# Summing weighted rows on VectorE ahead of one matmul per 512 columns, in the modulation rows of a two-block kernel

## The chip, the cores and the metric

The kernel runs on one core of one Trainium2 chip. The metric is the device time of one execution in microseconds; "before" is the median of three runs. The profile is one further execution, recorded by the hardware profiler. Engines are named as the profile does: PE (matrix multiply), DVE (VectorE), ACT (ScalarE), POOL (GpSimd), SP (the engine that issues most transfers here).

## The reference

A first block of two hybrid layers is followed by a second block (gated linear attention, a state space mixer, a gated recurrence and a feed-forward net). The change touches only the adaptive layer norm of the first block:

```
mod = jax.nn.silu(c) @ ada_w + ada_b          # c: [1, 1024], ada_w: [1024, 3072] per layer
shift, scale, gate = jnp.split(mod, 3, axis=-1)
h = rms_norm(x, norm_g) * (1.0 + scale[:, None, :]) + shift[:, None, :]
proj = h @ w_in
...
return x + gate[:, None, :] * y
```

So for each layer one vector of 1024 numbers is multiplied with a matrix of 1024 x 3072, in float32, giving one row of 3072. Layer 0's shift and scale are computed at the start of the kernel by other code. What is left for later is the gate of layer 0 (1024 columns) and the whole row of layer 1 (3072 columns): eight pieces of 512 columns.

## The kernel before

`ada_rows` (lines 260 to 297) makes the eight later pieces. It returns a list of small jobs, one for each "round" and each block `k` of 128 rows of the matrix: layer 0's gate is one round of 8 jobs with one load each, layer 1 has a round of 8 jobs with two loads each and one of 8 jobs with one load each, 32 loads of 128x1024 (512 KB) in all. A job loads its block into the tile `adaw` (two buffers, line 283) and multiplies each half of 512 columns with the column `self.sc[:, k:k+1]` (128 entries of silu(c)) as a matmul with one output row (line 285). The eight matmuls of a piece accumulate in a PSUM tile `adr`, on partition 32*g. In the last job of a round the row is read by VectorE, the bias is added (line 292), for layer 1's scale also the gain is applied (line 294), and the row goes to DRAM (line 296). Two later matmul records in the profile stand for each float32 matmul.

`hybrid` (from line 402) hands these jobs to layer 0 only (`prep`). They are put one after each job of the second projection stage: chunk "NV" (8 tiles of 128 tokens), "DV" (8 tiles, 256 columns) and "DQ" (8 tiles, 512 columns). A DQ tile (`job_df`, line 744) is 24 matmuls into `pj`, a copy `dr` by ScalarE (three buffers), squares, a sum (line 758), an inverse square root in three Newton steps on VectorE (lines 117 to 123), a scaling (line 762), a rotation in four operations on VectorE for one half and on POOL for the other (`rope`, lines 340 to 343), four transposes on PE into `dfTp` (line 770), and a split into two parts by ScalarE and VectorE (`sgd`, line 774) that goes to DRAM (`dfT`).

After this come the sixteen gate tiles (`gate_tile`, line 605): 24 matmuls into `pg`, a tanh on ScalarE into `gth` (line 612; three buffers), a multiply on VectorE that reads `pg` again (line 613), and a store to `gTd` by SP. `pj` and `pg` share one PSUM tag of two banks. Then attention loads its operands (`md`, line 920, and `ml`, line 866) and starts.

The program's order on each engine is not the order of the code: a scheduler places instructions by its own estimate of their times, and each engine then runs its queue strictly in that order. A weight block is loaded into `raw`, rounded by ScalarE into `wh`, and the rest `wl` is subtracted by VectorE for even blocks and by POOL for odd ones (`load_wt`, lines 153 to 163).

Of the kernel before, what the change touches and what calls it, by code (L numbers as in the profile page):

```python
# [12 lines left out]
F32 = mybir.dt.float32  # L13
# [3 lines left out]
ALU = mybir.AluOpType  # L17
# [35 lines left out]
class Kern:  # L53
# [206 lines left out]
    def ada_rows(self, li, pool, tag, dst, nbuf, rnds=(0, 1)):  # L260

        nc, a = self.nc, self.a
        X = {}

        def step(rnd, k):
            ng = 4 if rnd == 0 else 2
            if k == 0:
                X["p"] = self.ps(tag, f"adr{rnd}")[:, 0:512]
                X["b"] = pool.tile([128, 512], F32, name="brow", tag="brow", bufs=1)
                X["rows"] = pool.tile([128, 512], F32, name="rows", tag="rows", bufs=1)  # L270
                for g in range(ng):
                    ci = rnd * 4 + g
                    nc.scalar.dma_start(X["b"][32 * g:32 * g + 1, :], a["ada_b"][li:li + 1, ci * 512:ci * 512 + 512])
                if rnd == 0:
                    X["n"] = pool.tile([128, 512], F32, name="ngr", tag="ngr", bufs=1)
                    for g in range(2):
                        nc.scalar.dma_start(X["n"][64 + 32 * g:65 + 32 * g, :],
                                            a["norm_g"][li:li + 1, g * 512:g * 512 + 512])
            pr = X["p"]
            for h in range(0, ng, 2):  # L280
                w = pool.tile([128, 1024], F32, name="adaw", tag="adaw", bufs=nbuf)
                c0 = (rnd * 4 + h) * 512
                nc.sync.dma_start(w, a["ada_w"][li, k * 128:(k + 1) * 128, c0:c0 + 1024])
                for g in (h, h + 1):
                    nc.tensor.matmul(pr[32 * g:32 * g + 1, :], self.sc[:, k:k + 1],
                                     w[:, (g - h) * 512:(g - h + 1) * 512], start=k == 0, stop=k == 7)
            if k < 7:
                return
            rows = X["rows"]
            for g in range(ng):  # L290
                sl = slice(32 * g, 32 * g + 1)
                nc.vector.tensor_tensor(rows[sl, :], pr[sl, :], X["b"][sl, :], ALU.add)
                if rnd == 0 and g >= 2:
                    nc.vector.scalar_tensor_tensor(rows[sl, :], rows[sl, :], 1.0, X["n"][sl, :], ALU.add, ALU.mult)
                ci = rnd * 4 + g
                nc.scalar.dma_start(dst[ci:ci + 1, :], rows[sl, :])
        return [lambda r=r, k=k: step(r, k) for r in rnds for k in range(8)]

    def mod_bc(self, pool, mod, which, name):
# [2118 lines left out]
```

## Time and profile before

| | |
|---|---|
| median of 3 runs | 2950.08 us (2942.32 to 2954.98) |
| profiled execution | 2954.67 us, span 2952.9 us |
| PE busy | 2734.3 us (93%) |
| VectorE busy | 1924.0 us (65%) |
| ScalarE busy | 1299.9 us (44%) |
| POOL busy | 1114.3 us (38%) |
| the jobs' matmuls | 128 records, 251.1 to 386.2 us |
| last gate tile of layer 0 | tanh at 427.19 us |

The page gives shares over the whole span; the change lies in a stretch of some 180 us near its start. For that stretch one asks the trace for busy times by window, for the queue of one engine in order of time, and for what each instruction waited for (the square brackets at the end of a row). A matmul record can be longer than the distance to the next one, since matmuls are pipelined; distances between starts are what a matmul costs.

### The profile page before, as it was taken

Reading aid. Unit: us, or ns where it says so; the run is one execution under the profiler, and the core shown is the slowest. Engines: PE = TensorE matmul, PEld = TensorE weight load, DVE = VectorE, ACT = ScalarE, POOL = GpSimd, SP = SyncE. Lnnn points to the kernel's source line nnn. Section 1 sums busy time; section 2 is a strip of 40 time slices with the busy share of each in tenths; the row PEclk is TensorE's granted clock in tenths of the full one; section 3 lists DMA queues with packets and bytes.
Section 4 is the critical chain, followed back from the end, with each engine's and each line's share of the span. In section 5 each row is a group of like instructions: output and inputs, shape, how many; then the busy total and the mean of one; then the engine's idle time right before and its main releaser. Section 6 shows DMA issues by size and latency. Waiting matters only on the chain. (4 is left out here: it accounts for less than half of the span.)

```text
span 2952.9 us, 42552 instructions
## 1 busy us (share of the span) xinstructions
PE 2734.3 (93%) x14954; PEld 2186.5 (74%) x14954; DVE 1924.0 (65%) x4245; ACT 1299.9 (44%) x2542; POOL 1114.3 (38%) x849
## 2 busy tenths in 40 slices
PE   7999999998998999989999998999995989999899
PEld 6987666666778997766767775798673767787687
DVE  4784628785577677267865568643678888776733
ACT  5552227675623643166766323224233323333544
POOL 2232216662221324145742114342204665333743
PEclk9999999999999999989999998899996999999899
DMA  7456661435573363434056742235521555323963
GB/s 225 113 135 211 206 177 69 107 91 151 181 264 99 89 179 100 140 107 117 27 148 187 247 125 71 85 108 193 174 99 64 185 193 188 107 97 124 318 194 109
DMA packets 316602, 428.66 MB, mean 145 GB/s; under 512 B 36658, under 2 KB 224162, under 8 KB 314980
## 3 DMA queue, kind: packets, MB, share of 16 engines
q1 hardware_dynamic: 294464, 367.96, 41.4%
q10 hardware_dynamic: 21924, 57.98, 5.1%
q8 instruction: 118, 1.93, 0.3%
q14 instruction: 96, 0.79, 0.1%
HBM read 292.60 MB, written 132.64 MB: 144 GB/s over the span
## 5 line engine op out<-in xcount | busy, mean ns | idle before, releaser
L794 ACT ACTIVATE P<-P,nb 128x1024 f32<-128x1024 f32 (+1 forms) x320 | 316.5, 990 | 122.8 <-DVE nb L787 94.1
L127 PE MATMUL pj<-wh,hh 128*128 128x384 f32 (+3 forms) x768 | 265.4, 347 | 1.1 <-ACT cr L624 0.5
L128 PE MATMUL pj<-wl,hh 128*128 128x384 f32 (+3 forms) x768 | 264.2, 345 | 0.0
L129 PE MATMUL pj<-wh,hl 128*128 128x384 f32 (+3 forms) x768 | 261.7, 345 | 0.0
L806 PE MATMUL ptp<-ident,P 128*128 128x128 f32 x1568 | 220.3, 279 | 10.0 <-ACT PT L808 6.3
L806 PEld LDWEIGHTS ptp<-ident,P 128*128 128x128 f32 x1568 | 182.0, 143 | 52.0 <-issue 19.9
L954 POOL TENSOR_TENSOR P<-P,cf 128x1024 f32<-128x1024 f32 x64 | 121.8, 1906 | 211.7 <-DVE cf L952 164.6
L2035 POOL TENSOR_TENSOR fwl<-wraw,fwh 128x1024 fp32r<-128x1024 f32 (+1 forms) x66 | 150.2, 2278 | 134.1 <-ACT fwh L2034 126.9
L162 POOL TENSOR_TENSOR wl<-raw,wh 128x384 fp32r<-128x384 f32 (+3 forms) x64 | 77.3, 1212 | 296.7 <-ACT wh L161 253.7
L808 ACT COPY PT<-ptp 128x512 f32<-128x512 f32 (+1 forms) x255 | 138.1, 554 | 72.8 <-PE ptp L806 55.8
L787 DVE CUSTOM_DVE_ANT_0 P<-sd,zero 128x1024 f32<-128x1024 f32 x128 | 153.8, 1216 | 22.0 <-PE sd L945 21.8
L127 PE MATMUL po<-wh,yh 128*128 128x512 f32 x384 | 153.2, 406 | 8.6 <-ACT yh L1548 4.9
L129 PE MATMUL po<-wh,yl 128*128 128x512 f32 x384 | 151.9, 402 | 3.7 <-DVE yl L1549 3.7
L128 PE MATMUL po<-wl,yh 128*128 128x512 f32 x384 | 154.2, 402 | 0.8 <-DVE wl L140 0.5
L955 POOL TENSOR_TENSOR P<-P 128x1024 f32<-128x1024 f32 x64 | 153.5, 2401 | 3.6
L128 PEld LDWEIGHTS pj<-wl,hh 128*128 128x128 f32 x768 | 146.9, 191 | 10.7 <-issue 6.0
L127 PEld LDWEIGHTS pj<-wh,hh 128*128 128x128 f32 x768 | 146.9, 191 | 8.1 <-issue 0.9
L129 PEld LDWEIGHTS pj<-wh,hl 128*128 128x128 f32 x768 | 145.5, 190 | 8.0 <-issue 3.5
L2034 ACT CAST fwh<-wraw 128x512 fp32r<-128x512 f32 (+1 forms) x110 | 86.7, 791 | 142.1 <-PE fu L128 74.5
L787 DVE CUSTOM_DVE_ANT_0 P<-sm,zero 128x1024 f32<-128x1024 f32 x96 | 116.9, 1218 | 48.0 <-PE sm L129 42.8
L2253 DVE TENSOR_TENSOR dxl<-drx,dxh 128x512 fp32r<-128x512 f32 x75 | 77.3, 1054 | 100.3 <-ACT dxh L2252 94.4
L2253 POOL TENSOR_TENSOR dyl<-dry,dyh 128x512 fp32r<-128x512 f32 x75 | 109.5, 1475 | 87.6 <-ACT dyh L2252 87.5
(698 smaller groups left out, 7750.3 us busy)
## 6 DMA issues: line engine op xcount, KB each, us to landing
adaw<-in_ada_w_dram SPq DMA_DIRECT2D x48, 512.0 KB
wraw<-in_w_up_dram SPq DMA_DIRECT2D x22, 1024.0 KB
raw<-in_w_in_dram SPq DMA_DIRECT2D x76, 256.0 KB
drx<-fx SPq DMA_DIRECT2D x75, 256.0 KB
mn<-naT SPq DMA_DIRECT2D x72, 256.0 KB
nab<-in_na_rpb_dram SPq DMA_DIRECT2D x24, 576.0 KB
naT<-sgn SPq DMA_DIRECT2D x64, 192.0 KB
md<-dfT SPq DMA_DIRECT2D x96, 128.0 KB
```

The source lines that it names most:

```text
L127: mm(o, lh, rh, start=first, stop=False, **kw)
L128: mm(o, lh, rl, start=False, stop=False, **kw)
L129: mm(o, ll, rh, start=False, stop=last, **kw)
L787: nc.vector.tensor_tensor_reduce(out=P[:, :n], in0=src, in1=self.zero.to_broadcast([128, n]), op0=ALU.add, op1=ALU.min, scale=1.0, scalar= ...
L794: nc.scalar.activation(P[:, :n], P[:, :n], AF.Exp, bias=nb, scale=-1.0 if bias is None else 1.0, accum_out=sums)
L806: nc.tensor.transpose(T[:, j * 128:(j + 1) * 128], P[:, (c + j) * 128:(c + j + 1) * 128], self.ident)
L808: e(PT[:, c:c + m, q, :], T[:, 0:m * 128].rearrange("p (k t) -> p k t", k=m))
L954: nc.gpsimd.tensor_tensor(Ps[1], Ps[1], cf[:, 1:2].to_broadcast([128, S]), ALU.mult)
L955: nc.gpsimd.tensor_tensor(Ps[0], Ps[0], Ps[1], ALU.add)
L2034: nc.scalar.copy(wh, raw)
L2035: (eng or nc.gpsimd).tensor_tensor(wl, raw, wh.bitcast(F32), ALU.subtract)
L2253: eng.tensor_tensor(lo, raw, hi.bitcast(F32), ALU.subtract)
```

## The change

Each loaded block is multiplied by its 128 entries of `self.sc` on VectorE, one number for each partition, and summed into a tile `adac` of 128x1024: the first block of a round by a product, the next seven by a multiply-and-add. When a round's eight blocks are summed, one matmul with a column of ones for each 512 columns sums over the 128 partitions. `adac` has two buffers of 4 KB a partition. The loads, their buffers and what follows the row are the same.

```diff
+                X["a"] = [pool.tile([128, 1024], F32, name="adac", tag="adac", bufs=2) for _ in range(0, ng, 2)]
             pr = X["p"]
             for h in range(0, ng, 2):
                 w = pool.tile([128, 1024], F32, name="adaw", tag="adaw", bufs=nbuf)
                 c0 = (rnd * 4 + h) * 512
                 nc.sync.dma_start(w, a["ada_w"][li, k * 128:(k + 1) * 128, c0:c0 + 1024])
-                for g in (h, h + 1):
-                    nc.tensor.matmul(pr[32 * g:32 * g + 1, :], self.sc[:, k:k + 1],
-                                     w[:, (g - h) * 512:(g - h + 1) * 512], start=k == 0, stop=k == 7)
+                z = X["a"][h // 2]
+                if k == 0:
+                    nc.vector.tensor_scalar_mul(z, w, self.sc[:, 0:1])
+                else:
+                    nc.vector.scalar_tensor_tensor(z, w, self.sc[:, k:k + 1], z, ALU.mult, ALU.add)
             if k < 7:
                 return
+            for g in range(ng):
+                nc.tensor.matmul(pr[32 * g:32 * g + 1, :], self.ones, X["a"][g // 2][:, g % 2 * 512:g % 2 * 512 + 512],
+                                 start=True, stop=True)
```

In the changed file the lines behind this place are six higher (the gate multiply, 613 before, is 619). Three places show how the order moved.

VectorE, in the middle of the DQ tiles, before: the end of one tile's Newton steps, its rotation, and the next tile's sum.

```order
L762 TENSOR_TENSOR dr<-dr,rsd 128x512
L340 TENSOR_TENSOR rp_u<-dr,cg_dq 128x256
L341 TENSOR_TENSOR rp_w<-dr,sg_dq 128x8x16
L342 TENSOR_TENSOR rp_w<-dr,sg_dq 128x8x16
L758 TENSOR_REDUCE std<-jkd 128x16
L343 TENSOR_TENSOR dr<-rp_u,rp_w 128x256
L117 TENSOR_SCALAR std<-std 128x16
L118 TENSOR_SCALAR rsd<-std 128x16
```

VectorE, a rotation among the DQ tiles in the changed kernel (`adac` is the sum, `csc` the column of silu(c)).

```order
L289 SCALAR_TENSOR_TENSOR adac<-adaw,csc,adac 128x1024
L346 TENSOR_TENSOR rp_u<-dr,cg_dq 128x256
L347 TENSOR_TENSOR rp_w<-dr,sg_dq 128x8x16
L348 TENSOR_TENSOR rp_w<-dr,sg_dq 128x8x16
L123 SCALAR_TENSOR_TENSOR rsd<-nwt,rsd 128x16
L121 TENSOR_TENSOR nwt<-rsd 128x16
L289 SCALAR_TENSOR_TENSOR adac<-adaw,csc,adac 128x1024
L349 TENSOR_TENSOR dr<-rp_u,rp_w 128x256
```

The accumulations stand between the steps of one tile's rotation. Of the 32, eight stand ahead of the first DQ sum and 24 between it and the last rotation.

PE, where the gate tiles have begun, before: matmuls of the gates with one tile's transposes and two groups of the jobs' matmuls between them.

```order
L285 MATMUL adr_3097<-adaw,csc 1x512 x2
L770 MATMUL dfTp<-ident,dr 128x128 x4
L129 MATMUL pg<-hh,wl 128x512
L127 MATMUL pg<-hh,wh 128x512
L128 MATMUL pg<-hl,wh 128x512
L129 MATMUL pg<-hh,wl 128x512
L285 MATMUL adr_3097<-adaw,csc 1x512 x2
```

PE, the end of the second gate tile and the start of the third in the changed kernel.

```order
L129 MATMUL pg<-hh,wl 128x512
L776 MATMUL dfTp<-ident,dr 128x128 x8
L293 MATMUL adr_3453<-adac,ones 1x512 x2
L776 MATMUL dfTp<-ident,dr 128x128 x4
L127 MATMUL pg<-hh,wh 128x512
```

The last three DQ tiles' transposes now stand together behind two whole gate tiles, and all other gate matmuls behind them.

VectorE at the end of the same stretch, before: the last tile's rotation and split, and the first gate multiplies.

```order
L762 TENSOR_TENSOR dr<-dr,rsd 128x512
L340 TENSOR_TENSOR rp_u<-dr,cg_dq 128x256
L341 TENSOR_TENSOR rp_w<-dr,sg_dq 128x8x16
L342 TENSOR_TENSOR rp_w<-dr,sg_dq 128x8x16
L343 TENSOR_TENSOR dr<-rp_u,rp_w 128x256
L774 TENSOR_TENSOR sgd<-dfTp,sgd 128x512
L613 SCALAR_TENSOR_TENSOR gth<-gth,pg 128x512 x2
L774 TENSOR_TENSOR sgd<-dfTp,sgd 128x512
```

VectorE there in the changed kernel.

```order
L768 TENSOR_TENSOR dr<-dr,rsd 128x512
L298 TENSOR_TENSOR rows<-adr_3453,brow 1x512 x2
L346 TENSOR_TENSOR rp_u<-dr,cg_dq 128x256
L347 TENSOR_TENSOR rp_w<-dr,sg_dq 128x8x16
L348 TENSOR_TENSOR rp_w<-dr,sg_dq 128x8x16
L349 TENSOR_TENSOR dr<-rp_u,rp_w 128x256
L780 TENSOR_TENSOR sgd<-dfTp,sgd 128x512
L619 SCALAR_TENSOR_TENSOR gth<-gth,pg 128x512 x7
```

The last round's bias is now added ahead of the last rotation, and the gate multiplies begin only behind the last tile's split; before, two of them stood ahead of it.

SP, the loads for attention among the stores of the gate tiles, before.

```order
L158 DMA raw<-in_w_in_dram 128x512
L614 DMA gTd_86<-gth 128x512
L920 DMA md<-dfT_88 32x1024 x24
L866 DMA ml<-qTd_84 96x1024 x2
L866 DMA ml<-kTd_85 96x1024 x2
L614 DMA gTd_86<-gth 128x512 x7
```

SP, the same loads in the changed kernel.

```order
L284 DMA adaw<-in_ada_w_dram 128x1024 x4
L782 DMA dfT_88<-sgd 128x4x128 x6
L926 DMA md<-dfT_88 32x1024 x24
L872 DMA ml<-qTd_84 96x1024 x2
L872 DMA ml<-kTd_85 96x1024 x2
L620 DMA gTd_86<-gth 128x512 x7
```

All stores of gate tiles now stand behind the 28 loads; before, eight of the sixteen stood ahead of them.

## Rows read from the trace of the kernel before

**Rows 1.** The page, busy time of the engines, with share and instructions.

```profile
PE 2734.3 (93%) x14954; PEld 2186.5 (74%) x14954; DVE 1924.0 (65%) x4245; ACT 1299.9 (44%) x2542; POOL 1114.3 (38%) x849
```

**Rows 2.** Busy time by window, layer 0; columns as the first row says.

```profile
core 0: us, PE busy (x) PEld busy (x) DVE busy (x) ACT busy (x) POOL busy (x), PEclk, DMA share, GB/s
290.00:330.00 40.00, 40.00 (x177) 24.79 (x175) 36.67 (x104) 12.59 (x22) 18.94 (x24) 1.00 0.76 227
```

**Rows 3.** Instructions on tile adr: count, nanoseconds (least, median, most), first and last start.

```profile
L285 PE MATMUL adr<-adaw,csc x128: 590/591/592, 251.1 to 386.2; 128*1 128x512 f32 x128
```

**Rows 4.** PE in order of time: start, length, engine, line, operation, tiles, count.

```profile
250.77 0.28 PE L128 MATMUL pj<-wl,hh 128*128 128x256 f32 x1
250.89 0.28 PE L129 MATMUL pj<-wh,hl 128*128 128x256 f32 x1
251.10 1.03 PE L285 MATMUL adr<-adaw,csc 128*1 128x512 f32 x4
...
252.28 0.28 PE L128 MATMUL pj<-wl,hh 128*128 128x256 f32 x1
```

**Rows 5.** DVE in order of time, layer 1's DQ tiles; brackets: idle before, releaser.

```profile
1129.76 0.69 DVE L758 TENSOR_REDUCE std<-jkd 128x16 f32<-128x512 f32 x1 [5.42 <-ACT jkd L756]
...
1183.88 0.56 DVE L343 TENSOR_TENSOR dr<-rp_u,rp_w 128x256 f32<-128x256 f32 x1
...
1186.43 0.69 DVE L774 TENSOR_TENSOR sgd<-dfTp,sgd 128x512 fp32r<-128x512 f32 x1 [0.19 <-ACT sgd L773]
```

**Rows 6.** Busy time by window, layer 1's DQ tiles.

```profile
1130.00:1140.00 10.00, 10.00 (x45) 8.26 (x44) 9.80 (x36) 1.85 (x3) 4.27 (x7) 1.00 0.00 1
...
1160.00:1170.00 10.00, 7.04 (x33) 5.19 (x32) 9.62 (x22) 3.06 (x7) 5.99 (x6) 1.00 0.33 89
```

**Rows 7.** DVE groups by form: count, busy us, mean ns, idle before.

```profile
L1615 DVE SCALAR_TENSOR_TENSOR rgm<-rgm,rtr 128x1024 f32<-128x1024 f32 x12 | 14.6, 1220 | 0.2
...
L1597 DVE SCALAR_TENSOR_TENSOR xc<-xr,convw,xc 128x1024 f32<-128x1024 f32 x6 | 10.5, 1754 | 0.1
...
L209 DVE TENSOR_SCALAR xs<-xs,xrs 128x1024 f32<-128x1024 f32 x4 | 2.8, 751 | 0.1
```

**Rows 8.** SP in order of time, the third and fourth load.

```profile
252.16 2.79 SPq L283 DMA_DIRECT2D adaw<-in_ada_w_dram  x2
```

**Rows 9.** Busy time by window beside it; the last number is GB/s, or KB.

```profile
253.00:254.00 1.00, 1.00 (x10) 0.52 (x8) 0.00 (x0) 0.00 (x0) 0.00 (x0) 1.00 0.69 143
254.00:255.00 1.00, 1.00 (x8) 0.49 (x5) 0.07 (x1) 0.00 (x0) 0.00 (x0) 1.00 0.91 356
```

**Rows 10.** DVE in order of time, layer 0's first DQ sum.

```profile
269.16 0.69 DVE L758 TENSOR_REDUCE std<-jkd 128x16 f32<-128x512 f32 x1 [4.41 <-ACT jkd L756]
```

**Rows 11.** Instructions on tile rows, the bias additions.

```profile
L292 DVE TENSOR_TENSOR rows<-adr,brow x8: 672/683/697, 280.5 to 387.6; 1x512 f32<-1x512 f32 x8
```

**Rows 12.** ACT in order of time, tanh of gate tiles, layer 0 and layer 1.

```profile
427.19 0.60 ACT L612 ACTIVATE gth<-pg 128x512 f32<-128x512 f32 x1 [4.84 <-PE pg L129]
...
1193.29 0.60 ACT L612 ACTIVATE gth<-pg 128x512 f32<-128x512 f32 x1 [6.89 <-PE pg L129]
...
1212.29 0.60 ACT L612 ACTIVATE gth<-pg 128x512 f32<-128x512 f32 x1 [7.53 <-DMA gTd<-gth]
...
1264.02 0.60 ACT L612 ACTIVATE gth<-pg 128x512 f32<-128x512 f32 x1 [4.85 <-PE pg L129]
```

**Rows 13.** SP in order of time, layer 1's loads for attention and the stores behind.

```profile
1190.27 11.83 SPq L920 DMA_DIRECT2D md<-dfT  x24
...
1204.46 12.25 SPq L614 DMA_DIRECT2D gTd<-gth  x5
```

**Rows 14.** DVE in order of time, two 16-column operations in layer 0.

```profile
316.41 0.17 DVE L117 TENSOR_SCALAR std<-std 128x16 f32<-128x16 f32 x1
316.62 1.24 DVE L118 TENSOR_SCALAR rsd<-std 128x16 int32<-128x16 int32 x1
```

**Rows 15.** POOL in order of time, beside them.

```profile
316.53 3.07 POOL L162 TENSOR_TENSOR wl<-raw,wh 128x512 fp32r<-128x512 f32 x2 [2.08 <-ACT wh L161]
```

## The prediction

> **What bounds the kernel now.** I read the page first, then stage windows, then single queues. PE is busy for 93% of the span [rows 1], and in the stage of the change it has no gap: from 290 to 330 us it is busy 40.00 of 40 us, but VectorE is busy 36.67 of 40 in the same stretch [rows 2]. The reader should see both numbers, since the work goes from the first engine to the second just there. The stage is layer 0's last projections: eight "DV" tiles, eight "DQ" tiles (24 matmuls each, then a long VectorE chain that scales and rotates the tile) and sixteen gate tiles. The 64 one-column matmuls leave 128 records there [rows 3].
>
> A control stands in the same trace. Layer 1 runs the same tiles with no modulation work beside them. There the first reduction of the DQ chain starts at 1129.76 and the last rotation ends at 1183.88 + 0.56 = 1184.44, which is 54.7 us [rows 5]; VectorE is busy 9.80 and 9.62 of 10 us in two of these slices, and PE only 7.04 of 10 in the second [rows 6]. So with the modulation matmuls gone, this stretch is already VectorE's. In layer 0 those matmuls lie in time that PE would else partly wait. That is the base of the forecast.
>
> **What is removed and added on PE.** Ordinary matmuls start 0.12 us apart (250.77, 250.89); with one group of four records between them, the matmul two places after 250.89 starts at 252.28, 1.39 us later instead of 0.24, so a group costs 1.15 us [rows 4]. 128 records are 32 such groups: 36.8 us of PE. Eight matmuls with ones come back, 16 records or four such groups: 4.6 us. If PE set the end all along, the kernel would gain 32 us.
>
> **What is added on VectorE.** 32 operations on 128x1024. Twenty-eight multiply-and-add with two SBUF inputs; the nearest row of that shape, alone, is 1.22 us, and the same form beside a busy POOL 1.754 [rows 7]. Four are a first product, like the row of 0.751 [rows 7]. Where they stand decides: the new order puts eight of them ahead of the DQ chain and 24 (21 and 3) between its instructions, and both PE's last set of transposes, ahead of the third gate tile, and VectorE's first gate multiply come after all of them.
>
> Start of the chain. The first loads were in use at 251.10 [rows 4]; I put the first accumulation at 250. With two buffers a load is issued when the accumulation two before it is done. The third load was issued at 252.16 and its 524 KB came by about 255.1 (143 KB to 254, 356 KB to 255, the rest after) [rows 8, 9], so a buffer's turn is 2.9 + 1.22 + 0.2 for issue and semaphores = 4.3 us, 2.15 per load. Seven more take 15, and the last operation is done at about 266.6 (250 + 0.75 + 7 x 2.15 = 265.8, and the weight splits share the queue). Before, the chain began at 269.16 [rows 10]: PE reaches the DQ tiles earlier, but their chain gains only 2.6 us.
>
> Length of the chain to the last rotation: 54.7 as in layer 1; one more split of a transposed tile in front of it, 0.68; 21 x 1.22 = 25.6; 3 x 0.75 = 2.3; ten one-row operations that add bias and gain, 10 x 0.68 = 6.8 [rows 11], which in layer 0 partly stood later, beside idle VectorE. Sum 90.0. The long operations fill gaps between dependent short ones, which I put at -3 (bounds 0 and -9, an estimate: 88 short steps of 0.17 us each, as the 16-column row of [rows 14], with up to 0.1 hidden): 87. The last rotation ends at 266.6 + 87 = 353.6.
>
> From there to the end of the gates: in layer 1 the last gate's tanh starts at 1264.02, which is 79.6 after the last rotation; this holds two gate tiles done ahead, fourteen after it, and a slow first one (tanh at 1193.29, 8.9 after the rotation) [rows 12]. There the first gate multiply went just ahead of the last split; in the new order it comes behind it. That split ended at 1186.43 + 0.69 = 1187.12 [rows 5], 2.7 after the rotation: +2.7. SP also issues 24 loads "md" and four "ml" ahead of every store of a gate tile; in layer 1 two stores went ahead of them. These issues took 14.2 us (1190.27 to 1204.46) [rows 13], so with three gate buffers the fourth tanh waits. Worked through from the rotation: the loads start 3.15 after the split as in layer 1 (1190.27), at 5.9; the first store is issued at 20.1 and has landed at 23.0 (2.9 as the load above); tanh and multiply, about 0.6 and 0.7, free the bank at 24.3. PE wants it after the third of its late gate tiles, at 8.85 + 2.7 + 2 x 5.44 = 22.4 (5.44 is a thirteenth of 1193.29 to 1264.02). It loses 1.9 us; bounds 0 and 5. In layer 1 a tanh waited 7.53 us for such a store [rows 12] and PE lost nothing. Total 84.2, so the last tanh starts at 437.8. Before it was 427.19 [rows 12]. The change costs 10.6 us.
>
> What follows, attention, starts from the last gate and its loads in both versions; I carry no gain or loss there. Loads as such are no limit: 32 at 2.15 us end at 319, and PE no longer waits behind them. The eight matmuls with ones are late by a hop or two behind their accumulations, but their readers stand 5 us further on in VectorE's queue; cost nothing while VectorE is behind, 1 us each round if not.
>
> The profiled execution took 2954.67 us around its span of 2952.9; the median of the three runs is 2950.08, 4.6 lower. The sum is a difference and is put on the median: 2950.1 + 10.6 = 2961.
>
> **The rivals.** First, PE as the limit: the accumulations hide and the time is 2950 - 32 = 2918. For it speaks that PE shows no gap in layer 0; against it that layer 1's PE has gaps in the same work without any accumulations. VectorE would have to end its chain by 266.6 + 54.7 = 321 in spite of 35 us of added operations. Even a chain of 72 us gives -4 (266.6 + 72 + 84.2 = 422.8), not -15.
>
> Second, slower: the accumulations and POOL hold each other up. A 16-column VectorE operation took 1.24 us from 316.62, where its like just before took 0.17, while POOL ran two subtractions from 316.53 on, 3.07 us for both [rows 14, 15]. POOL rotates the other half of every DQ tile and splits odd weight blocks, 18.94 of 40 us here [rows 2]. At 1.754 each, 21 accumulations take 11.2 more: 2950.1 + 10.6 + 11.2 = 2972, and 2978 with a 5 us store wait and no filling of gaps. It decides from an average of 1.42 us per accumulation (21 x 0.20 = 4.2 us more, +14.8 in all). For it speaks the same-form row at 1.754; against it that part of POOL's hold-up is already inside layer 1's 54.7 us.
>
> The Trainium skill, page "SBUF — State Buffer", section "SBUF: two separate sides", says that VectorE operations with two SBUF inputs and GpSimd operations that read SBUF take one port pair in turn, each for its whole instruction, the later one blocked. By that rule the second rival would be the outcome, near its 2972, since every accumulation has two SBUF inputs; the record of 1.24 us, ending about when the first POOL subtraction does, agrees with it, while the filled slices of layer 1 show that the loss is not on every operation.
>
> **How the numbers follow.** A measurement of this kernel can tell about 0.5%, 14.8 us, from no change. The forecast (+2 to +14 us, 2952 to 2964) has 0.60; the slower rival (2965 to 2978) 0.33; PE as the limit, and anything else below 2935, 0.07. Hence slower 0.33, same 0.60, faster 0.07. Bounds: a chain of 81 and no store wait gives 266.6 + 81 + 82.3 = 429.9, +3; a chain of 101 and 5 us of store wait gives 454.9, +28. With some 6 us below for the spread of the runs (2942 to 2955) the range is 2946 to 2978.
>
> **What would show it.** Right: VectorE over 95% busy from about 268 to 350; PE with some 30 us of gaps there that end on VectorE's rotation or split; the last rotation near 354; mean accumulation 1.2 to 1.4 us; the last tanh near 438; attention as long as before. Wrong: PE without gaps to the end of the gates (first rival); accumulations at 1.5 us and more (second); VectorE waiting for "adaw" loads, which would mean that a load takes far over 2.9 us; or an end of the gates as forecast and a different length of attention.

## The result and the profile after

The changed kernel takes 2970.95 us (median of 4 runs, 2967.06 to 2972.94) against 2949.7 before: ratio 1.0075, 95% interval 1.0058 to 1.0092. It is slower by 21 us, inside the range and on the side forecast, but twice the 11 us predicted. It lies outside the 2952 to 2964 that had the largest chance (0.60), in the band of the second rival (0.33) and at that rival's number. Its profiled span is 2970.9 us, 18.0 more than before.

The page's busy times, for [rows 1]:

```profile
PE 2715.0 (91%) x14842; PEld 2190.0 (74%) x14842; DVE 1954.8 (66%) x4277; ACT 1300.9 (44%) x2542; POOL 1121.9 (38%) x849
```

PE lost 19 us of work and the kernel got 21 us longer. The stage by windows (columns as in [rows 2]); the last line is the whole stretch from the first DQ sum to the last rotation:

```profile
300.00:320.00 20.00, 14.16 (x56) 10.52 (x54) 20.00 (x38) 4.54 (x8) 11.18 (x11) 0.90 0.70 204
...
340.00:360.00 20.00, 4.75 (x15) 2.03 (x16) 18.76 (x38) 1.17 (x2) 8.83 (x12) 0.58 0.56 158
...
273.36:359.23 85.87, 56.14 (x218) 39.03 (x216) 81.34 (x182) 16.29 (x28) 34.45 (x36) 0.83 0.71 209
```

Where [rows 2] had PE full, VectorE is now the full engine (81.34 of 85.87 us, 95%) and PE stands still for 29.7 us. VectorE in order of time, at both ends of the chain, for [rows 5, 10]:

```profile
272.15 1.28 DVE L289 SCALAR_TENSOR_TENSOR adac<-adaw,csc,adac 128x1024 f32<-128x1024 f32 x1 [3.02 <-DMA adaw<-in_ada_w_dram]
273.36 0.68 DVE L764 TENSOR_REDUCE std<-jkd 128x16 f32<-128x512 f32 x1
...
358.81 0.42 DVE L349 TENSOR_TENSOR dr<-rp_u,rp_w 128x256 f32<-128x256 f32 x1
361.17 0.69 DVE L780 TENSOR_TENSOR sgd<-dfTp,sgd 128x512 fp32r<-128x512 f32 x1 [1.93 <-ACT sgd L779]
```

The chain runs from 273.36 to 359.23: 85.9 us, where layer 1 took 54.7. PE's waits there and just behind:

```profile
345.52 1.18 PE L776 MATMUL dfTp<-ident,dr 128*128 128x128 f32 x4 [6.94 <-DVE dr L349]
352.54 1.09 PE L776 MATMUL dfTp<-ident,dr 128*128 128x128 f32 x4 [5.83 <-DVE dr L349]
...
359.38 1.08 PE L776 MATMUL dfTp<-ident,dr 128*128 128x128 f32 x4 [3.88 <-DVE dr L349]
365.84 0.79 PE L127 MATMUL pg<-hh,wh 128*128 128x512 f32 x1 [5.37 <-DVE gth L619]
...
386.61 0.50 PE L127 MATMUL pg<-hh,wh 128*128 128x512 f32 x1 [1.90 <-DVE gth L619]
```

PE waits for each rotated tile although fourteen gate tiles are left to do: they come later in its queue. The tanh of gate tiles on ScalarE, for [rows 12]:

```profile
364.47 1.09 ACT L618 ACTIVATE gth<-pg 128x512 f32<-128x512 f32 x2 [3.33 <-DMA dfT<-sgd]
...
385.24 1.25 ACT L618 ACTIVATE gth<-pg 128x512 f32<-128x512 f32 x2 [10.78 <-DMA gTd<-gth]
...
448.39 0.60 ACT L618 ACTIVATE gth<-pg 128x512 f32<-128x512 f32 x1 [4.84 <-PE pg L129]
```

The last tanh is at 448.39; before it was at 427.19: 21.2 us, the whole loss. Behind it the rest of the kernel takes 2522.5 us of the span against 2525.7 (2952.9 - 427.2), so attention shows no loss. The first row matters: two gate tiles, whose matmuls were done by 338.6, stand behind the last DQ tile's copy and then wait 3.33 us more for a *store of a DQ tile*. The gate buffer must lie in memory that the DQ stage used.

### The profile page after: what moved, and what is told of

Its sections match the earlier page's. It is cut to its first block, busy times and chain, and to the rows that moved or that the text cites. A ratio compares the mean times of both kernels' runs of the same rounds, so it can differ in the third digit from the quotient of the medians.

```text
span 2970.9 us, 42365 instructions
## 1 busy us (share of the span) xinstructions
PE 2715.0 (91%) x14842; PEld 2190.0 (74%) x14842; DVE 1954.8 (66%) x4277; ACT 1300.9 (44%) x2542; POOL 1121.9 (38%) x849
## 5 line engine op out<-in xcount | busy, mean ns | idle before, releaser
L793 DVE CUSTOM_DVE_ANT_0 P<-sd,zero 128x1024 f32<-128x1024 f32 x128 | 153.9, 1216 | 23.0 <-PE sd L951 22.4
```

The source lines that it names most:

```text
L793: nc.vector.tensor_tensor_reduce(out=P[:, :n], in0=src, in1=self.zero.to_broadcast([128, n]), op0=ALU.add, op1=ALU.min, scale=1.0, scalar= ...
```

## The experiments

The theory after the first reading: the price is VectorE's time in the DQ stage, plus waits for loads ahead of it, plus waits at the gate buffers. Its rivals: VectorE and POOL hold each other up; the loads set the pace. All runs in one table; times in the stage are of the profiled execution, the last rotation by its end.

| kernel | median us | ratio to before (95%) | first DQ sum | last rotation | last tanh |
|---|---|---|---|---|---|
| before | 2949.7 | 1 | 269.2 | 333.4 | 427.2 |
| changed | 2970.95 | 1.0075 (1.0058 to 1.0092) | 273.4 | 359.2 | 448.4 |
| no_jobs | 2919.48 | 0.9908 (0.9891 to 0.9924) | 266.5 | 322.2 | 399.5 |
| late24 | 2938.05 | 0.9968 (0.9955 to 0.9981) | 266.8 | 324.5 | 417.8 |
| bufs3 | 2969.49 | 1.0071 (1.0057 to 1.0086) | 270.0 | 356.0 | 445.4 |
| gth_own | 2948.21 | 1.0002 (0.9993 to 1.0010) | 271.2 | 358.3 | 427.3 |
| own3 | 2947.24 | 1.0005 (0.9990 to 1.0019) | 270.1 | 357.5 | 426.5 |
| before_own | 2948.00 | 0.9995 (0.9981 to 1.0010) | 268.8 | 333.0 | 426.8 |
| half | 2939.76 | 0.9977 (0.9967 to 0.9987) | 272.5 | 351.7 | 422.0 |
| late24_own | 2930.98 | 0.9953 (0.9940 to 0.9966) | 265.4 | 323.3 | 415.1 |
| late24_own_pe | 2968.50 | 1.0070 (1.0053 to 1.0086) | 270.6 | 329.7 | 424.7 |
| late24_own_q | 2946.33 | 1.0001 (0.9987 to 1.0015) | 273.2 | 329.5 | 420.6 |
| late24_own_pool | 2943.54 | 0.9989 (0.9977 to 1.0001) | 267.1 | 324.0 | 417.9 |
| no_rope_own | 2941.35 | 0.9976 (0.9962 to 0.9989) | 269.9 | 352.7 | 420.7 |

**What the jobs cost at all (no_jobs).** In the changed kernel:

```diff
-                nc.sync.dma_start(w, a["ada_w"][li, k * 128:(k + 1) * 128, c0:c0 + 1024])
...
-                    nc.vector.scalar_tensor_tensor(z, w, self.sc[:, k:k + 1], z, ALU.mult, ALU.add)
...
-                nc.vector.tensor_tensor(rows[sl, :], pr[sl, :], X["b"][sl, :], ALU.add)
+                nc.vector.tensor_copy(rows[sl, :], X["b"][sl, :])
```

> Leaves out the loads, the products, the sums and the matmuls with ones; the rows are the bias alone. VectorE theory (the forecast's: VectorE's queue sets the length of the DQ stage, and PE fills or waits): the chain from the first DQ sum to the last rotation takes 55 us as in layer 1 (it was 64 in the kernel before and 86 in the changed one) and starts at about 263; the last gate tanh comes 80 to 84 us after the last rotation, at 398 to 402, against 427 before and 448 in the changed kernel: about 2921 to 2925 us, with gaps on PE of some 10 us or more in the DQ stage. PE theory (PE set the end in the kernel before): all 36.8 us of its one-row matmuls are gained and PE has no gaps: 2913 us. Hold-up theory (VectorE and POOL delay each other because of the added sums): VectorE's hold-ups fall with the sums, mean of the rotation's rows below layer 1's.

VectorE's first DQ sum and last rotation, in layer 0:

```profile
266.46 0.69 DVE L749 TENSOR_REDUCE std<-jkd 128x16 f32<-128x512 f32 x1 [5.56 <-ACT jkd L747]
...
321.32 0.91 DVE L334 TENSOR_TENSOR dr<-rp_u,rp_w 128x256 f32<-128x256 f32 x1
```

55.8 us: the control of layer 1 holds in layer 0, though the chain starts at 266.5 and not at about 263. The last tanh comes 77.3 us later, and the kernel takes 2919 us, between the two theories (2921 to 2925, and 2913) and nearer to VectorE's. So the jobs cost 28 us on PE and some 50 us on VectorE; the base of the forecast stands.

**The sums behind the DQ chain (late24).** Layer 1's 24 loads multiply a copy of the column that is made from the last rotated tile (times zero, plus the column):

```diff
+            if L["late"] and t == NT - 1:
+                nc.vector.scalar_tensor_tensor(self.scl, r[:, 0:8], 0.0, self.sc, ALU.mult, ALU.add)
...
-            side_jobs = prep(WB) if prep else []
+            side_jobs = prep(WB)[:8] if prep else []
...
+                    for _ in range(1):
+                        if late:
+                            late.pop(0)()
```

> The 24 loads' sums of layer 1's two rounds take a copy of the column that is made after the last DQ rotation, so they stand behind it, beside the gate tiles; the first round stays where it is. VectorE theory: the chain starts at about 273 as in the changed kernel and takes 55 to 58 us; the last rotation is at about 330, the last gate tanh 80 to 90 us later, with three groups of 1.15 us of the matmuls with ones: 413 to 421, or 2936 to 2944 us, faster than the kernel before. Hold-up theory: the same direction, since POOL is idle beside the gates; the late sums take 1.28 us each. Load theory (the 32 loads set the pace wherever they are): the loads collide with attention's loads and the stores of the gate tiles, and the time stays at 2965 us or more.

As VectorE's theory said: the chain takes 57.7 us, and the kernel beats the one before. The load theory's 2965 is out. The start is 266.8, not 273: only six of the eight sums stand ahead of the first DQ sum here. The gates took 93.3 us, because PE waited for gate multiplies (waits of PE; us in total, times, longest):

```profile
PE pg L127 <- DVE gth L626: 10.7, 4, 5.3
```

**The loads (bufs3).**

```diff
-                prep = None if last else lambda P: (K.ada_rows(0, P, "U", mods[0], 2, (1,)) +
-                                                    K.ada_rows(1, P, "U", mods[1], 2))
+                prep = None if last else lambda P: (K.ada_rows(0, P, "U", mods[0], 3, (1,)) +
+                                                    K.ada_rows(1, P, "U", mods[1], 3))
```

> Three buffers for the loaded blocks in place of two. VectorE theory: only the waits for loads go, 6.3 us ahead of the first DQ sum and 2.4 us behind it in the changed kernel's trace; the first DQ sum moves from 273.4 to about 268, the chain stays near 84 us: 2963 to 2967 us. Load theory: the pace of the whole stage is the loads', and a third buffer gives 10 us or more: 2960 us or less. Hold-up theory: no more than 2 us: 2969 to 2971.

The first sum moved forward by 3.4 us and the last tanh by 3.0, half of what was expected, and the time by 1.5 us, which this measurement does not tell from nothing. By its time, 2969.49, the run falls in the range of the hold-up theory and not in that of VectorE's, so it rules out only the load theory. In the profiled execution the stretch behind the last tanh is 3.8 us longer than in the changed kernel (2526.3 against 2522.5), but that execution lies 4.0 us above its median, so a loss there is not shown.

**The gate buffers (gth_own, own3, before_own).** Six buffers (three in own3) in a pool on the other side of the memory, which no DQ tile used; before_own is the same edit in the kernel before:

```diff
-        with self.pool(f"gt{li}", not side) as GT:
+        with self.pool(f"gt{li}", not side) as GT0:
+            GT = near.enter_context(self.pool(f"go{li}", side))
...
-        th = W.tile([128, 512], F32, name="gth", tag="gth", bufs=3)
+        th = W.tile([128, 512], F32, name="gth", tag="gth", bufs=6)
```

> The gate tiles' buffers are six in place of three and lie in memory that no earlier tile of the stage used. In the changed kernel the first gate tanh behind the chain waited 3.33 us for a store of the tiles before, and a later one 10.78 us for a gate store, PE losing 1.90 us. If these two waits are the 5 us by which the gates took longer than forecast (89.2 us from the last rotation to the last tanh, against 84.2): 2965 to 2967 us, with about 84 us. If the time is PE's slower clock after the gap, or the gates hang on another wait: 2970 to 2971.

A miss that explains the case: not 5 us came back but all 21, and the chain on VectorE is as long as ever (87.1 us). What changed is PE's order. In the changed kernel 48 of the 384 gate matmuls stand ahead of the last transposes; here 140. PE's transposes and its one long wait in that stretch:

```profile
347.85 0.60 PE L777 MATMUL dfTp<-ident,dr 128*128 128x128 f32 x4
...
355.38 0.60 PE L777 MATMUL dfTp<-ident,dr 128*128 128x128 f32 x4
...
359.60 0.38 PE L777 MATMUL dfTp<-ident,dr 128*128 128x128 f32 x2
...
387.88 0.79 PE L127 MATMUL pg<-hh,wh 128*128 128x512 f32 x1 [7.94 <-ACT wh L161]
```

No bracket at the three transposes: PE comes to them from gate matmuls, where it had waited 6.94, 5.83 and 3.88 us; the 5.37 us behind them are gone too, 22.0 us in all. What it lost later is a late weight block. To tell the place from the number of buffers:

> Three gate buffers as in the changed kernel, but in memory of their own. Place theory: the six buffers of their own gave 21 us because gate tiles no longer wait for memory of the DQ tiles and run beside the DQ chain (140 gate matmuls ahead of the last transposes in PE's order, 48 in the changed kernel's; this kernel has the 140 too): 2946 to 2952 us. Number theory: it was the number of buffers: 2965 to 2971.

> The kernel before with the six gate buffers in memory of their own; its PE order is unchanged. Place theory: PE has no gap in this stage, so there is nothing to win: 2944 to 2950 us. If the buffers are worth 21 us by themselves, whatever VectorE does: 2926 us.

Both came as the place theory said. With three buffers it is 2947.24 us; in the kernel before the edit does nothing, since PE had no gap to fill.

**Half the VectorE work (half).**

```diff
-                    nc.vector.scalar_tensor_tensor(z, w, self.sc[:, k:k + 1], z, ALU.mult, ALU.add)
+                    nc.vector.scalar_tensor_tensor(z, w[:, 0:512], self.sc[:, k:k + 1], z, ALU.mult, ALU.add)
```

> Products and sums over the first 512 of the 1024 loaded columns alone, with all loads and all matmuls with ones (which read the one half twice). VectorE theory: 21 sums of about 0.68 in place of 1.33 us and three products at half inside the chain take 14 to 15 us off it; the last rotation at about 344, the last tanh at 434 in place of 448: 2955 to 2958 us. Load theory: the loads are the same and set the pace: 2967 to 2971.

The time fell by 31 us, twice the expectation, while the last rotation moved by 7.5. VectorE now waits for loads in the chain (waits of VectorE; us, times, longest), which takes half of the saving:

```profile
DVE adac L289 <- DMA adaw<-in_ada_w_dram: 8.7, 10, 1.5
```

The rest is again PE's order: 103 gate matmuls stand ahead of the last transposes, and no gate tanh waits for a store of a DQ tile any more. The edit also halves `adac`, which can move the tiles placed behind it in that memory; whether the shorter sums or the place let the gates ahead is not separated here. So this run does not give the price of a sum. Beside own3, whose gates also run ahead, it does better: a chain 8 us shorter is worth 7.5 us, in two different orders.

**Both together (late24_own, late24_own_pe).** The late sums and the six gate buffers; then the same two edits in the kernel before, with its one-column matmuls on PE.

> The sums of layer 1's rounds behind the last rotation and six gate buffers of their own. In the first of these alone the gates took 93 us, with 10.7 us of PE waiting for gate multiplies behind stuck stores, where a kernel without the jobs needs 77. If VectorE's queue in the DQ stage and the gate buffers were the whole price: chain of 55 to 58 us, last tanh at 402 to 408, 2921 to 2929 us. If the late loads themselves delay attention's loads and the stores: 2934 us or more.

> The place alone: the kernel before's one-column matmuls on PE, with layer 1's two rounds behind the last rotation and six gate buffers of their own. If late sums won 17 us because VectorE has room beside the gates and PE has none: 24 groups of 1.15 us come back beside the gates and three groups of matmuls with ones go, 24 us more than with the sums on VectorE, less the waits for loads there: 2942 to 2956 us. If the place was what won: 2931 us.

2930.98 us, the fastest version here, between the two expectations: 17 us under the kernel before, and some 11 above the kernel without the jobs. The waits of PE for gate multiplies are left:

```profile
PE pg L127 <- DVE gth L627: 10.0, 3, 6.5
```

With PE's matmuls in that place it is 2968.50, above the expected range; some of them come behind the last gate tile (tanh at 424.7; the last jobs' matmuls run to 440 us), and PE also waits 7.0 us for loads. The place alone is a loss, VectorE in that place a gain. Of the 17 us some 12 lie in the stage (last tanh 415.1 against 427.2); where the others lie stays open.

**What is left (late24_own_q, late24_own_pool).** Two tries at those 10 us, both on late24_own, the second with three gate buffers in place of six:

```diff
-                nc.sync.dma_start(w, a["ada_w"][li, k * 128:(k + 1) * 128, c0:c0 + 1024])
+                (nc.gpsimd if li else nc.sync).dma_start(w, a["ada_w"][li, k * 128:(k + 1) * 128, c0:c0 + 1024])
```

```diff
-        nc.vector.scalar_tensor_tensor(th, th, 1.0, p, ALU.add, ALU.mult)
+        pc = W.tile([128, 512], F32, name="gpc", tag="gpc", bufs=3)
+        nc.scalar.copy(pc, p)
+        nc.gpsimd.tensor_tensor(th, th, pc, ALU.mult)
+        nc.gpsimd.tensor_tensor(th, th, pc, ALU.add)
```

> As the kernel with the late sums and the six gate buffers, but layer 1's 24 loads are issued by POOL, not SP. There PE waited 10.0 us for gate multiplies, which stood on VectorE behind sums that waited for loads, and those loads stood on SP behind attention's 24 loads and the gates' stores. If SP's order is the cause: the waits go, the last gate tanh comes at 405 to 410 in place of 415: 2921 to 2927 us. If the transfers' rate is the limit (24 loads of 512 KB beside attention's loads, stores and weights): 2929 to 2933 us.

> The late sums again, with the gate multiply taken off VectorE in both layers: ScalarE copies the gate tile out of PSUM after its tanh and POOL multiplies and adds in SBUF (three buffers each for tanh and copy, in memory of their own). With the multiply on VectorE PE waited 10.0 us for it, behind sums that waited for loads. If that queue is what is left of the price: these waits go, the last gate tanh comes at 404 to 408 in place of 415, and layer 1 does not change: 2920 to 2926 us. If the stores of the gate tiles behind attention's loads hold the buffers all the same, or POOL's two operations are too slow: 2929 us or more.

The first missed both of its ranges. Its 24 loads issued by POOL land in a median of 4.6 us (at most 9.9) against 4.0 (at most 4.6) from SP, PE's waits for gate multiplies fall only to 6.0 us, and a weight block comes 4.7 us late: from the last rotation to the last tanh it is 91.1 us, where late24_own took 91.8. So taking the loads out of SP's order did not win the stretch. The rest of its loss is not explained: its DQ chain starts 7.8 us later. The second came out on the side of its second theory, 2929 us or more: with the multiply on POOL the three buffers hang on stores behind attention's 24 loads. Whether six buffers would have helped was not tried. ScalarE's tanh and PE's matmul behind it:

```profile
367.16 0.60 ACT L626 ACTIVATE gth<-pg 128x512 f32<-128x512 f32 x1 [14.46 <-DMA gTd<-gth]
```

```profile
368.29 0.80 PE L127 MATMUL pg<-hh,wh 128*128 128x512 f32 x1 [13.31 <-ACT gpc L628]
```

So the store wait, which cost PE 1.90 us in the changed kernel, can cost 13. How to win the last 11 us or so stays open.

**The hold-ups (no_rope_own).** own3 without POOL's rotation:

```diff
-            self.rope(nc.gpsimd, W, d3[:, 8:16], L["cdk"], L["sdk"], 8, t, "k")
```

> The changed kernel with three gate buffers of their own, and without POOL's rotation of the second half of the DQ tiles, which leaves out part of the computation; the order on PE is the same but for pairs of transposes. Hold-up theory: the delays on VectorE that go with POOL are some 13 us in the DQ stage by the trace (short operations of 0.17 us that took 0.7 to 1.4) and are as large in layer 1, without any sums; without POOL's rotation most of it goes, and the chain takes 75 to 78 us in place of 87; if they are on the path that sets the end, the time falls by 10 us to 2937. VectorE and gates theory: the chain is shorter all the same, but the gates' end is set by PE and the late weight load: 2943 to 2949.

The chain took 82.7 us, 4.7 less than own3's 87.4, not 10, and the time fell by 6 us, to 2941.35, below the one theory's range and above the other's 2937. The two chains by window, own3 first (columns as in [rows 2]):

```profile
270.10:357.50 87.40, 74.37 (x310) 55.69 (x309) 81.08 (x184) 18.81 (x32) 34.34 (x36) 0.92 0.70 212
```

```profile
269.90:352.70 82.80, 72.41 (x307) 54.17 (x306) 73.64 (x184) 18.81 (x32) 8.04 (x4) 0.94 0.74 227
```

VectorE has as many operations and is busy for 7.4 us less (81.08 - 73.64); longer waits for loads and matmuls take 2.5 us of that back (7.8 and 1.9 us against 6.2 and 1.0). VectorE's groups in the chain, first here, then in the changed kernel, then in layer 1 of the kernel before, which has no sums (columns as in [rows 7]):

```profile
L289 DVE SCALAR_TENSOR_TENSOR adac<-adaw,csc,adac 128x1024 f32<-128x1024 f32 x22 | 29.1, 1325 | 7.9 <-DMA adaw<-in_ada_w_dram 7.8
...
L121 DVE TENSOR_TENSOR nwt<-rsd 128x16 f32<-128x16 f32 x24 | 3.7, 169 | 0.1
...
L349 DVE TENSOR_TENSOR dr<-rp_u,rp_w 128x256 f32<-128x256 f32 x8 | 3.3, 417 | 0.0
```

```profile
L289 DVE SCALAR_TENSOR_TENSOR adac<-adaw,csc,adac 128x1024 f32<-128x1024 f32 x22 | 29.2, 1329 | 5.4 <-DMA adaw<-in_ada_w_dram 5.4
L121 DVE TENSOR_TENSOR nwt<-rsd 128x16 f32<-128x16 f32 x24 | 6.5, 281 | 0.1
L349 DVE TENSOR_TENSOR dr<-rp_u,rp_w 128x256 f32<-128x256 f32 x8 | 4.9, 615 | 0.0
L122 DVE SCALAR_TENSOR_TENSOR nwt<-nwt,std 128x16 f32<-128x16 f32 x24 | 4.8, 214 | 0.1
L123 DVE SCALAR_TENSOR_TENSOR rsd<-nwt,rsd 128x16 f32<-128x16 f32 x24 | 4.3, 191 | 0.0
```

```profile
L343 DVE TENSOR_TENSOR dr<-rp_u,rp_w 128x256 f32<-128x256 f32 x8 | 5.7, 710 | 0.0
L122 DVE SCALAR_TENSOR_TENSOR nwt<-nwt,std 128x16 f32<-128x16 f32 x24 | 5.4, 229 | 0.5
L121 DVE TENSOR_TENSOR nwt<-rsd 128x16 f32<-128x16 f32 x24 | 5.4, 229 | 0.6
L123 DVE SCALAR_TENSOR_TENSOR rsd<-nwt,rsd 128x16 f32<-128x16 f32 x24 | 4.6, 195 | 0.5
```

POOL's rotation does delay VectorE (a step of 169 ns becomes 229 to 281), but the 72 steps take 15.6 us with the sums (6.5 + 4.8 + 4.3) and 15.4 without (5.4 + 5.4 + 4.6), the four operations of VectorE's rotation even less with them (17.0 against 20.4, the last one 4.9 against 5.7). And the sums took 1325 ns without POOL's rotation and 1329 with it. So the hold-ups were there before, and these rows show no more of them with the sums.

## Why the prediction was right in range and sign, and short by half

- **Inside the range, in part by luck.** The upper end of the range was drawn for a chain of 101 us and a store wait of 5. Neither came (85.9 and 1.90 us); what filled that room were a late start of the chain and a slow start of the gates.
- **PE is not the limit once its matmuls go: right.** PE's gaps in the chain are 29.7 us (some 30 said), VectorE is 95% busy, and the first rival's 2918 is near what the kernel without jobs takes (2919), not this one.
- **Start of the chain, 266.6 forecast, 273.36 measured: 6.8 us, mis-sized.** The step was "a buffer's turn is 2.9 + 1.22 + 0.2". It took the landing of a load with little beside it. With weight blocks on the same queue the eighth load, issued at 266.31, was used at 272.15: 5.8 us. A sign of being wrong that the prediction named did show: VectorE waited for "adaw" loads, 9.9 us in eight waits. A third buffer took 3.4 of the 6.8 us away. The rows below are SP's queue there, where the weight loads follow at once, and the window, in which the DMA engines are 97% busy (columns as in [rows 2]).

```profile
266.31 0.33 SPq L284 DMA_DIRECT2D adaw<-in_ada_w_dram  x1
266.91 1.51 SPq L158 DMA_DIRECT2D raw<-in_w_in_dram  x2
```

```profile
266.30:272.15 5.85, 5.85 (x28) 4.84 (x27) 2.13 (x2) 2.09 (x4) 1.29 (x1) 1.00 0.97 351
```

- **Length of the chain, 87 forecast, 85.9 measured: right, in part by luck.** The number of the sums is as forecast. Their price in the chain is 1.33 us (1.22 in the sum, 1.2 to 1.4 said), 2.3 us more for 21 of them; and VectorE stands still for 4.5 us (85.87 - 81.34), 2.4 of them for loads, where layer 1's 54.7 us held 2.2 (54.68 - 52.45). So what filled gaps save, put at 3 us, must be some 9 (a difference, which holds the smaller hold-ups of the rotation too), the far end of the bounds, and the three errors cancel.
- **From there to the last tanh, 84.2 forecast, 89.2 measured: 5.0 us, one wait missing and one price short.** PE's gap behind the gate store is 1.90 us, the number that was worked out, but by luck: behind the rotation, the tanh that needs the store comes at 26.0 us (23.0 said; the store, issued at 377.33, took 7.9 us and not 2.9), and PE asks for the bank at 25.5 (22.4 said). Both are 3 us late. Not foreseen: the tanh that waits 3.33 us for a DQ store, since its buffer lies on that tile's memory. PE so starts 6.6 us behind the rotation, where layer 1's 1.0 and the forecast 2.7 made 3.7. And PE runs at half its clock for some 4 us behind a gap: once in layer 1, twice here (below).
- These three (6.8 - 1.1 + 5.0 = 10.7) make up the difference between 10.6 us forecast and 21.2 measured at the last tanh.
- **What the sum took as given** lies under it: that what the chain is late, the gates are late. For this kernel, whose order the prediction had before it, that held. But layer 1's "two gate tiles done ahead, fourteen after it" is no property of the work; own3 shows it to be one of the order on PE: with gate buffers in other memory the chain is as late as before, and the end is 22 us earlier. The order rows ahead of the prediction showed it too ("behind two whole gate tiles"), but it was read as a given and not as a price.
- **The second rival had the number (2972), and its mechanism fell.** It wanted 1.754 us a sum and decided from 1.42 on; the mean of all 28 is 1.37, and the hold-ups with POOL are no larger with the sums than without. By the Trainium skill's page "SBUF — State Buffer", section "SBUF: two separate sides", a VectorE operation with two SBUF inputs and a POOL operation that reads SBUF lock each other out, whichever starts first, for its whole length. The delays that vanish with POOL's rotation agree with such a lock (the steps of 169 ns have two inputs). The row of 1.24 us [rows 14], which the prediction put beside that rule, is no such case: that operation has one input. And VectorE did not pay for more of it. POOL's 36 operations of the chain show 34.45 us in the changed kernel (the window above) and 27.20 in layer 1 of the kernel before (its window below); spans on POOL are rough, but by them it was POOL that lost, and POOL had room (34.45 of 85.87 us).

```profile
1129.76:1184.44 54.68, 46.82 (x217) 37.55 (x215) 52.45 (x147) 17.30 (x30) 27.20 (x36) 0.99 0.34 97
```

## What to carry to other kernels

Work that moves from a full engine to one that looks free has to be priced in the stage where it lands, and the price depends on what the first engine can do meanwhile: look whether independent work stands behind the wait in its queue, and what keeps it there; here it was a buffer's place in memory, worth 22 us. A control in the same trace (the same stage without the moved work) gave the length of the new chain well, with errors that cancelled, but it hands on its own order and its own hidden limits, which have to be asked after separately. Here the move paid only together with a move of its place: the sums on VectorE cost 21 us in the DQ stage, and with 24 of the 32 loads' sums beside the gates (and the gate buffers moved) the kernel won 17; VectorE had been busy there for 19.5 of 93.8 us.

## What the runs showed of the hardware

After a gap PE can come back at half its clock. Windows of the changed kernel from 365.8 on, behind the 5.37 us gap; the last three numbers are granted clock, DMA share and GB/s:

```profile
365.80:370.20 4.40, 4.36 (x10) 3.47 (x11) 0.59 (x1) 0.00 (x0) 0.00 (x0) 0.50 0.94 240
371.00:384.00 13.00, 13.00 (x59) 10.73 (x58) 0.69 (x1) 0.60 (x1) 0.00 (x0) 1.00 1.03 250
```

0.50 is 1.2 GHz, 1.00 is 2.4: ten matmuls in the first window, 4.5 a microsecond in the second. The gap of 1.90 us before 386.61 was followed by the same (387.6 to 391.0, nine matmuls in 3.4 us, where 4.5 a microsecond would make 2.0), after about a microsecond at full clock: here a short gap cost nearly as much again as it is long. Not each gap did so: after one of 1.16 us before 332.85 the granted clock stayed at 1.00 to 338.6. Loads of 512 KB took from 3.4 to 6.2 us to land in late24_own (median 4.3), where [rows 8, 9] gave 2.9: a landing read beside few other transfers is a lower bound.
